# A two-layer decoder trunk on one core: one block-wise gate and up group, later sums, and a new order at the start of the first mixer

## The chip, the core and the metric

The kernel runs on one core of one Trainium2 chip. The core has a matrix engine, TensorE (PE in the profile; its weight loads are PEld), VectorE (DVE), ScalarE (ACT), GpSimd (POOL), and SyncE (SP), whose queue issues most of the transfers from and to HBM. The metric is the device time of one execution in microseconds (us); lower is better.

## What is computed

The input x has 256 tokens of 1024 columns, in float32. Two layers follow each other; each adds half a SwiGLU feed-forward network (FFN), a mixer, and half a second FFN, all on normed inputs. The first layer's mixer is dilated attention beside spatial gating, the second's is block-sparse attention. Cut to what matters here:

```python
def rms_norm(x, g):
    y = x * lax.rsqrt(jnp.mean(x * x, axis=-1, keepdims=True) + EPS)
    return y * g

def swiglu(x, w_gate, w_up, w_down):        # 1024 -> 2816 -> 1024
    return (jax.nn.silu(x @ w_gate) * (x @ w_up)) @ w_down

for layer in range(2):
    h = h + 0.5 * swiglu(rms_norm(h, ffn1_norm[layer]), ...)
    h = h + mixer[layer](rms_norm(h, mix_norm[layer]))
    h = h + 0.5 * swiglu(rms_norm(h, ffn2_norm[layer]), ...)
return rms_norm(h, final_norm)
```

## The kernel before

The code numbers six phases: 0 first FFN, 1 first mixer, 2 second FFN, 3 third FFN, 4 second mixer, 5 last FFN.

**Three products for one.** The matrix products must be as good as float32, so every operand is split in a high half (float32r, a rounded copy that ACT makes) and a low half (the rest, a subtraction on DVE). `mm3` (L388 to L391) then issues three products: high by high (L389), and the two mixed ones (L390, L391). Activations lie transposed, as `xTh` and `xTl`: 8 k tiles of 128 rows by 256 tokens. In a plain step the weights are stationary (128 x 128) and the 256 tokens move.

**The weight stream.** `weight_chunks` lists every piece of the weights in the order of use, and `Stream` brings them. A chunk has at most 2048 columns on 128 partitions (1 MB). SP loads it into one of three `raw` buffers (`load_one`, L202), ACT makes `whi` (L250) and DVE `wlo` (L257) in one of four pairs of buffers, and PE takes it (`take`) and gives it back (`free`). So a chunk can be split when PE has given back the one four places before it, and loaded when DVE has read the one three places before it. Where a chunk's `reset` is set, its first three k tiles are laid out with their column halves apart.

**An FFN.** The 2816 hidden columns are 11 groups of 256. Step n of 22 does the gate (n even) or up (n odd) columns of group n // 2: `colwise`, 2 column halves x 8 k tiles x 3 products. After every second step `gated` (L717 on) multiplies the gate by the row of inverse norms, applies SiLU, multiplies by up, and splits the result into `hTh` and `hTl`, 22 k tiles for the down projection that follows in 12 chunks.

**Blocks.** In phases 0, 3 and 5 part of the down projection runs by seven block products instead of eight, with sums of weight blocks (kind "S", formed by DVE at L264, L267 and L268 from the raw chunk) and sums of activation blocks (L739 to L741). There the weights move and 128 x 128 blocks of activations are stationary (`seven_products`). The last FFN's weight sums are formed ahead: `begin_sums` fetches a chunk into the tile `blocks` (L667), DVE forms three or four sums in place (L671 to L677), and `keep` stores them to HBM (L683). `AHEAD` names the steps of phases 2 and 3 at which the fetches are issued; the sums come one step after their fetch, and the store one step later. `blocks` has two buffers in phase 2.

**The start of a mixer.** `first_tiles` does four tiles of 256 columns: `LATE` (L537) is the order of the first two, `ps4[0]` and `ps4[1]`: six k tiles of the one, six of the other, then the last two of each. Four k tiles of `ps4[3]` follow, then (first mixer) `everywhere`: two products with ones (L482, L483) add the squares up, and a chain of DVE and ACT steps (mean L484, root L485, reciprocal L486, row L490) makes the row of inverse norms, by which `put_q` and `put_k` scale the queries and keys (L1068) for the first score (L1127). The next weight splits are tied behind the mean (`issue_after`).

The order of the instructions on each engine is drawn up by a scheduler at build time, by the order of the code and by what it takes to be ready; SP's queue works in order.

Of the kernel before, what the change touches and what calls it, by code (L numbers as in the profile page):

```python
# [10 lines left out]
F32 = mybir.dt.float32  # L11
# [4 lines left out]
S = 256  # L16
D = 1024
NT = S // 128
# [36 lines left out]
def weight_chunks():  # L55
# [11 lines left out]
    def ffn(name, layer, last=False, again=(2, 3), phase=None):  # L67
        first = len(chunks)
        wd = (f"{name}_w_down", layer)
        lag = LAGS.get(phase, FT)  # L70
        woven = phase in LAGS

        def seven(pair):
            add(wd, pair * 256, 2, 0, 512, MSHIFT, kind="S")

        for c in range(0, FF, 256):
            if len(chunks) == 0:
                for k in (0, 4):
                    add((f"{name}_w_gate", f"{name}_w_up", layer), k * 128, 4, c, c + 256, SHIFT,
                        (1, 2, 3) if k else (0.5, 1, 1.5, 2, 3))  # L80
                continue
            for m in ("gate", "up"):
                n = len(chunks)
                cuts = (6,) if first == 0 and n in again else ()
                cols((f"{name}_w_{m}", layer), c, 256, cuts,
                     RESET if n - first in again or woven and m == "gate" and c // 256 > lag else 0)
            if c // 256 >= lag:
                seven(c // 256 - lag)
        if last:
            for i in range(FT // 2):  # L90
                add(wd, i * 256, 2, 0, D, kind=LAST[i])
            return
        rest = list(range(FT // 2 - lag, FT // 2)) if woven else []
        behind = woven
        if lag > 2 and woven:
            seven(rest.pop(0))
        for c in range(512 if woven else 0, D, 256):
            for k, n in DOWN:
                add(wd, k * 128, n, c, c + 256, SHIFT, reset=RESET if behind or woven and lag == 2 and (c, k) == (768, 8) else 0)
                behind = bool(rest)  # L100
                if rest:
                    seven(rest.pop(0))
# [244 lines left out]
def trunk(ctx: ExitStack, tc: tile.TileContext, a, out):  # L347
# [311 lines left out]
    def begin_sums(fp, n):  # L659
# [29 lines left out]
    def ffn(phase):  # L689
        nonlocal nxt  # L690
        with tc.tile_pool(name="fp", bufs=1) as fp:
# [12 lines left out]
            else:  # L704
                parts = [fp.tile([128, S], F32R, name=n) for n in ("acch", "accl")]
                parts += [fp.tile([128, S], F32, name=n) for n in ("mean", "sqrt", "inverse")]

# [8 lines left out]

            ready, ahead = [], []  # L717

# [85 lines left out]
            for n in range(FT):  # L804
                k, m = n - n % 2, n % 2
                if phase == n == 0:
                    with tc.manual_schedule():
                        ready += begin(fp)
                elif phase or n > 1:
                    p = bank()  # L810
                    w = st.take()
                    colwise(p, w, *(() if n else (TURNS,)))
                    st.free()
                    ready.append(p)
                if phase == 2 and n == 1:

                    nc.tensor.matmul(bank()[:, :1], ones, ones[:, :1], start=True, stop=True)
                sums_at(n)
                if n == late - 1:
                    if phase not in (2, 5):  # L820
                        split(*parts[:2], nxt.acc[:, 0])
                    nxt.everywhere(*parts)
                    if last:
                        half = nxt.column(norm["half"], parts[3][:, :128], "halfcol")
# [7 lines left out]
                if n == late:  # L832
                    for i in range(0, n, 2):
                        gated(i, *ready[i : i + 2])
                elif n > late and m == 1:
                    gated(k, *ready[-2:])
# [386 lines left out]
    def first_tiles(put_q, put_k, step, places=None):  # L1223
# [11 lines left out]
        w = st.take()  # L1235
        tile_of(ps4[3], w, 1, range(4))
        if places:
# [7 lines left out]
        step()  # L1245
        tile_of(ps4[3], w, 1, range(4, KD))
        step()
# [164 lines left out]
def _layout(a):  # L1412
# [6 lines left out]
    for j, (ms, layer, r, n, c0, c1, *how) in enumerate(chunks):  # L1419
        w = np.concatenate([a[m][layer, r : r + n * 128, c0:c1] for m in ms], axis=1)  # L1420
        if j >= len(chunks) - FT // 2:
            w = w[:, ROWS]
        w = tiles(w)
        if how[-1] != "N":
# [38 lines left out]
```

## Time and profile before

| | |
|---|---|
| time, median of 3 runs | 919.52 us (919.25 to 919.65) |
| time of the profiled execution | 919.54 us |
| its span, first to last instruction | 917.8 us |
| mean granted TensorE clock | 0.999 |
| DMA, mean over the span | 220 GB/s, 202.17 MB |

The profile's page gives busy times by engine, a row of tenths over 40 equal slices of the span, the chain of work that ended last, and groups of instructions with count, busy time and mean duration. Products of PE are pipelined, so the duration of one (277 ns for 256 columns) is longer than the distance from one start to the next, and it is the distance that adds up.

### The profile page before, as it was taken

How to read it: one execution, taken by the hardware profiler on the slowest of the kernel's cores; microseconds unless marked ns; L12 is line 12 of the kernel's file. 1: busy time of each engine (PE TensorE's matmuls, PEld its weight loads, DVE VectorE, ACT ScalarE, POOL GpSimd, SP SyncE). 2: the span in 40 equal slices, each digit the busy share in tenths (PEclk: the TensorE clock that was granted, in tenths of full speed). 3: DMA queues.
4: the chain of work that ended last, by engine and by line, in shares of the span. 5: the costliest groups of instructions: out<-in, count | busy, mean ns of one | idle time of the engine just before them, and what ended most of it. 6: DMA issues, size and time to landing. Idle time of an engine off the chain costs nothing.

```text
span 917.8 us, 18462 instructions
## 1 busy us (share of the span) xinstructions
PE 910.5 (99%) x7531; PEld 891.8 (97%) x7531; DVE 774.5 (84%) x1267; ACT 561.9 (61%) x873; POOL 81.8 (9%) x117
## 2 busy tenths in 40 slices
PE   9999999999999999999999999999999999999997
PEld 9999999999999999999999999999999999999886
DVE  7999897997889777767799888878778799978897
ACT  7766555668667544444566555556777776555573
POOL 0000000034310000000000000001665100000001
PEclk9999999999999999999999999999999999999999
DMA  9656655665247779698746755575443566865691
GB/s 338 239 167 229 202 183 204 233 227 184 93 184 264 280 283 350 230 371 312 254 153 244 278 184 190 170 262 206 170 139 138 136 228 203 284 214 189 233 313 50
DMA packets 35428, 202.17 MB, mean 220 GB/s; under 512 B 4064, under 2 KB 6368, under 8 KB 14992
## 3 DMA queue, kind: packets, MB, share of 16 engines
q1 hardware_dynamic: 33840, 197.79, 60.4%
q0 software_dynamic: 496, 1.77, 0.9%
q10 hardware_dynamic: 1008, 1.44, 0.5%
q8 instruction: 59, 0.97, 0.4%
q14 instruction: 25, 0.20, 0.1%
HBM read 188.14 MB, written 12.85 MB: 219 GB/s over the span
## 4 chain that ended last, share of the span: by engine, by line
PE 99%; issue 0%; DVE 0%; POOLq 0%; POOL 0%; DVEq 0%
PE bank L391 31%; PE bank L389 31%; PE bank L390 31%; PE bank L1165 1%; PE bank L637 1%; PE bank L640 0%; PE bank L613 0%; PE bank L1127 0%; PE bank L1129 0%; PE bank L1128 0%; PE bank L923 0%; PE bank L919 0%; PE bank L920 0%; PE bank L1314 0%; PE bank L789 0%
## 5 line engine op out<-in xcount | busy, mean ns | idle before, releaser
L250 ACT ACTIVATE whi<-raw 128x1024 fp32r<-128x1024 f32 (+5 forms) x390 | 351.4, 946 | 227.1 <-PE bank L390 141.9
L257 DVE TENSOR_TENSOR wlo<-raw,whi 128x1024 fp32r<-128x1024 f32 (+5 forms) x390 | 414.5, 1091 | 36.1 <-ACT whi L250 34.9
L389 PE MATMUL bank<-xTh,whi 128*128 128x256 f32 x1600 | 442.8, 277 | 0.0
L390 PE MATMUL bank<-xTl,whi 128*128 128x256 f32 x1600 | 442.0, 276 | 0.0
L391 PE MATMUL bank<-xTh,wlo 128*128 128x256 f32 x1600 | 441.9, 276 | 0.0
L390 PEld LDWEIGHTS bank<-xTl,whi 128*128 128x128 f32 x1600 | 300.4, 188 | 0.2 <-DVE xTl L428 0.2
L389 PEld LDWEIGHTS bank<-xTh,whi 128*128 128x128 f32 x1600 | 300.4, 188 | 0.0
L391 PEld LDWEIGHTS bank<-xTh,wlo 128*128 128x128 f32 x1600 | 300.4, 188 | 0.0
L389 PE MATMUL bank<-hTh,whi 128*128 128x256 f32 x352 | 97.7, 278 | 0.0
L391 PE MATMUL bank<-hTh,wlo 128*128 128x256 f32 x352 | 97.3, 277 | 0.0
L390 PE MATMUL bank<-hTl,whi 128*128 128x256 f32 x352 | 97.3, 276 | 0.0
L390 PEld LDWEIGHTS bank<-hTl,whi 128*128 128x128 f32 x352 | 66.2, 188 | 0.0
L391 PEld LDWEIGHTS bank<-hTh,wlo 128*128 128x128 f32 x352 | 66.1, 188 | 0.0
L389 PEld LDWEIGHTS bank<-hTh,whi 128*128 128x128 f32 x352 | 66.1, 188 | 0.0
L724 DVE TENSOR_TENSOR hm<-gs,bank 128x512 f32<-128x512 f32 x44 | 29.9, 684 | 35.2 <-PE bank L391 35.0
L1060 POOL MEMSET k<- 64x256 f32 x12 | 3.3, 306 | 561.0 <-DVE x L439 560.8
L394 ACT ACTIVATE hSh<-gs 128x512 fp32r<-128x512 f32 (+1 forms) x31 | 18.6, 601 | 29.9 <-DVE gs L741 13.0
L389 PE MATMUL bank<-whi,hTh 128*128 128x256 f32 (+1 forms) x114 | 36.1, 316 | 0.0
L390 PE MATMUL bank<-wlo,hTh 128*128 128x256 f32 (+1 forms) x114 | 36.0, 316 | 0.0
L391 PE MATMUL bank<-whi,hTl 128*128 128x256 f32 (+1 forms) x114 | 36.0, 316 | 0.0
L389 PE MATMUL bank<-mixh,whi 128*128 128x256 f32 x128 | 35.7, 279 | 0.0
L721 DVE TENSOR_TENSOR gs<-bank,row 128x512 f32<-128x512 f32 x44 | 29.9, 686 | 6.9 <-PE bank L391 6.7
(247 smaller groups left out, 1308.7 us busy)
## 6 DMA issues: line engine op xcount, KB each, us to landing
raw<-in_weights SPq DMA_DIRECT2D x131, 1024.0 KB, 4.9
raw<-in_weights SPq DMA_DIRECT2D x28, 512.0 KB, 3.6
blocks<-in_weights SPq DMA_DIRECT2D x9, 1024.0 KB, 8.3
blocks<-blocks SPq DMA_DIRECT2D x9, 1024.0 KB, 7.2
raw<-blocks SPq DMA_DIRECT2D x7, 1024.0 KB, 4.8
raw<-in_weights SPq DMA_DIRECT2D x8, 768.0 KB, 5.0
raw<-in_weights SPq DMA_DIRECT2D x7, 256.0 KB, 4.8
blocks<-block SPq DMA_DIRECT2D x5, 256.0 KB, 8.9
```

The costliest lines, as they stand in the source:

```text
L250: done = nc.scalar.activation(hi, r, AF.Copy)
L257: self.made[u] = done, nc.vector.tensor_sub(lo, r, hi.bitcast(F32))
L389: nc.tensor.matmul(p, sh, mh, start=start, stop=False)
L390: nc.tensor.matmul(p, sh, ml, start=False, stop=False)
L391: return nc.tensor.matmul(p, sl, mh, start=False, stop=stop)
L394: return nc.scalar.activation(hi, src, AF.Copy), nc.vector.tensor_sub(lo, src, hi.bitcast(F32))
L637: nc.tensor.matmul(o, w[0][i][:, cs], xT[m][:, k], start=k == 0 and m == "h" and j % 2 == 0, stop=False)
L721: nc.vector.tensor_mul(g, both(pg), twice(norm["row"]))
L724: nc.vector.tensor_mul(hm, g, both(pu))
L1060: nc.gpsimd.memset(pair[j][o, 1].bitcast(F32), 0.0)
L1165: nc.tensor.transpose(tp[:, i * 128 : (i + 1) * 128], pr[:, i * 128 : (i + 1) * 128], ident)
```

## The change

The hidden group 7 of the second FFN goes by blocks. Its gate and up columns, once two chunks of 2048 columns, become four chunks of kind "S", each with two k tiles of gate and up side by side (1024 columns loaded). Its steps 14 and 15 become one call of `by_blocks`: for each of the four chunks seven `mm3` with the weights moving. The sums of activation blocks are made ahead by `forms` in steps 7 to 10, into parts of `hTh` and `hTl` that aren't used yet (`xS`). The result stands with tokens on the partitions; it is combined, gated by ACT with a column of norms (`token`), multiplied, transposed in 32 x 32 blocks by DVE, stored to HBM at step 16, loaded in the other layout at step 17, and split into `hT` at step 19. The next group's gate gets the layout of `reset`.

The sums for the last FFN come two steps behind their fetch, the store three steps behind. Their fetches move to other steps, `blocks` has one buffer, and four of the nine fetches use the tile `seven`, which also holds the block step's result and three scratch rows of `everywhere`.

In both mixers the last two k tiles of the first two tiles come in another order (`end_of`): first all products with the high half of the activations, then those with the low half. In the first mixer six k tiles of `ps4[3]`, not four, stand ahead of the products with ones.

```diff
-AHEAD = [(2, n) for n in (2, 5, 9, 12, 16, 19, 23, 26)] + [(3, 5)]
+AHEAD = [(2, n) for n in (1, 3, 6, 8, 16, 19, 22, 25)] + [(3, 5)]
+BORROWED = ((2, 3), (2, 8), (2, 19), (2, 25))
+BLOCKED = {2: (7,)}
...
+            if c // 256 in blocked:
+                for k in range(0, KD, 2):
+                    add((f"{name}_w_gate", f"{name}_w_up", layer), k * 128, 2, c, c + 256, MSHIFT, kind="S")
+                continue
...
-                     RESET if n - first in again or woven and m == "gate" and c // 256 > lag else 0)
+                     RESET if n - first in again or m == "gate" and (woven and c // 256 > lag or
+                                                                     c // 256 - 1 in blocked) else 0)
...
-    LATE = ((0, range(6)), (1, range(6)), (0, range(6, 8)), (1, range(6, 8)))
...
-        t = fp.tile([128, CH], F32, name="blocks", bufs=2 if AHEAD[n][0] == 2 else 1)
+        if AHEAD[n] in BORROWED:
+            t = fp.tile([128, 8, S], F32, name="seven").rearrange("p i s -> p (i s)")
+        else:
+            t = fp.tile([128, CH], F32, name="blocks")
...
+            def forms(i):
+
+                xg, t = (fp.tile([128, 2, S], F32, name="gs", bufs=2) for _ in range(2))
+                for j in range(2):
+                    nc.scalar.activation(xg[:, j], x1(2 * i + j), AF.Copy, scale=nxt.gain(2 * i + j))
+                f = t.rearrange("p i (t c) -> p (i t) c", t=2)
+                nc.vector.tensor_sub(f[:, :2], xg[:, 0].rearrange("p (t c) -> p t c", t=2), xg[:, :, 128:])
+                nc.vector.tensor_sub(f[:, 2], f[:, 1], xg[:, 0, :128])
+                nc.vector.tensor_add(f[:, 3], xg[:, 1, :128], f[:, 2])
+                split(*(h[:, i] for h in xS), f)
+
+            def by_blocks(m, n):
+
+                b = [bank() for _ in range(4)]
+                for c in range(KD // 2):
+                    w = st.take()
+                    a11, a12, a22 = [[xT[h][:, 2 * c + k, t * 128 : (t + 1) * 128] for h in "hl"]
+                                     for k, t in ((0, 0), (1, 0), (1, 1))]
+                    s3, s1, s2, s4 = ([h[:, c, i] for h in xS] for i in range(4))
+                    for (i, h), (sh, sl), q in (((2, 0), a11, 0), ((0, 0), a12, 2), ((1, 0), s4, 1), ((1, 1), a22, 6),
+                                                ((3, 0), s1, 3), ((0, 1), s2, 5), ((2, 1), s3, 4)):
+                        mm3(b[i][:, h * S : (h + 1) * S], sh, sl, w[0][q], w[1][q], c == h == 0,
+                            c == KD // 2 - 1 and (h == 1 or i == 3))
+                    if c < KD // 2 - 1:
+                        st.free()
+                t = fp.tile([128, 8, S], F32, name="seven")
+                nc.scalar.activation(t[:, 7], b[2][:, :S], AF.Copy)
+                nc.vector.tensor_add(t[:, 1:3], twice(t[:, 7]), both(b[0]))
+                nc.vector.tensor_add(t[:, 3], t[:, 2], b[2][:, S:])
+                nc.vector.tensor_sub(t[:, 0:6:5], twice(b[3][:, :S]), t[:, 2:4])
+                nc.vector.tensor_add(t[:, 4:7:2], t[:, 0:4:3], both(b[1]))
+                for i in range(NT):
+                    nc.scalar.activation(t[:, 1 + 5 * i], t[:, 1 + 5 * i], AF.Silu, scale=token[:, i : i + 1])
+                st.free()
+                nc.vector.tensor_mul(t[:, 2:4], t[:, 1:7:5], t[:, 4:6])
...
+                for i, f in ((2, store), (3, load), (5, take)):
+                    later[n + i] = f
...
             def sums_at(n):
 
+                if (phase, n - 2) in AHEAD:
+                    ahead[n - 2] = ahead[n - 2]()
+                if (phase, n - 3) in AHEAD:
+                    ahead.pop(n - 3)()
                 if (phase, n) in AHEAD:
-                    ahead.append(begin_sums(fp, AHEAD.index((phase, n))))
-                if (phase, n - 1) in AHEAD:
-                    ahead.append(ahead.pop()())
-                if (phase, n - 2) in AHEAD:
-                    ahead.pop()()
+                    ahead[n] = begin_sums(fp, AHEAD.index((phase, n)))
...
+                elif n // 2 in blocked:
+                    if m == 0:
+                        by_blocks(n // 2, n)
...
+                if n in later:
+                    later.pop(n)()
+                if blocked and 7 <= n < 11:
+                    forms(n - 7)
...
+    def end_of(ps, w, ks):
+
+        cs = [slice(j * 128, (j + 1) * 128) for j in range(2)]
+        for k in ks:
+            for j in range(2):
+                for m in range(2):
+                    nc.tensor.matmul(ps[j][:, :S], w[m][k][:, cs[j]], xT["h"][:, k], start=False, stop=False)
+        for k in ks:
+            for j in range(2):
+                nc.tensor.matmul(ps[j][:, :S], w[0][k][:, cs[j]], xT["l"][:, k], start=False, stop=k == KD - 1)
...
-        for j, ks in LATE:
-            tile_of(ps4[j], w, j, ks)
+        for j in range(2):
+            tile_of(ps4[j], w, j, range(6))
+        end_of(ps4, w, range(6, KD))
...
-        tile_of(ps4[3], w, 1, range(4))
+        ahead = 6 if places else 4
+        tile_of(ps4[3], w, 1, range(ahead))
...
-        tile_of(ps4[3], w, 1, range(4, KD))
+        tile_of(ps4[3], w, 1, range(ahead, KD))
```

More of the change, by code (lines that the diff above doesn't have):

```diff
@@ L705, in ffn @@
                 parts = [fp.tile([128, S], F32R, name=n) for n in ("acch", "accl")]
-                parts += [fp.tile([128, S], F32, name=n) for n in ("mean", "sqrt", "inverse")]
+                if phase in BLOCKED:
+                    seven = fp.tile([128, 8, S], F32, name="seven")
+                    parts += [seven[:, i] for i in range(3)]
+                else:
+                    parts += [fp.tile([128, S], F32, name=n) for n in ("mean", "sqrt", "inverse")]
             def turn_back(t):
@@ L715, in turn_back @@
                     nc.sync.dma_start(away[t], xn)
-            ready, ahead = [], []
+            ready, ahead, later = [], {}, {}
+            blocked = BLOCKED.get(phase, ())
+            xS = [h[:, FT - KD :].rearrange("p (i n) s -> p i n s", n=2).rearrange("p i n (t c) -> p i (n t) c", t=2)
+                  for h in hT]
+            def forms(i):
[7 more added lines that the diff above has]
+                split(*(h[:, i] for h in xS), f)
@@ new lines, in by_blocks, with store, load, take @@
+            def by_blocks(m, n):
[21 more added lines that the diff above has]
+                nc.vector.tensor_mul(t[:, 2:4], t[:, 1:7:5], t[:, 4:6])
+                flat = t.rearrange("p i s -> p (i s)")
+                turned, back = flat[:, 4 * S : 6 * S], flat[:, : 2 * S]
+                for i in range(NT):
+                    nc.vector.transpose(turned.rearrange("p (b t r) -> p b t r", t=NT, r=32)[:, :, i],
+                                        t[:, 2 + i].rearrange("p (b c) -> p b c", c=32))
+                kept = dram.tile([128, 512], F32, name=f"turned{phase}{m}")
+                def store():
+                    with tc.issue_after(st.last.ins):
+                        nc.sync.dma_start(kept, turned)
+                def load():
+                    for g in range(4):
+                        with tc.issue_after(st.last.ins):
+                            nc.sync.dma_start(back[32 * g : 32 * (g + 1)].rearrange("c (i f) -> c i f", i=4),
+                                              kept[:, 128 * g : 128 * (g + 1)].rearrange("(i c) f -> c i f", i=4))
+                def take():
+                    v = back.rearrange("p (i j t r) -> p j t i r", i=4, j=2, t=NT)
+                    for j in range(2):
+                        split(*(h[:, 2 * m + j].rearrange("p (t i r) -> p t i r", t=NT, i=4) for h in hT), v[:, j])
+                for i, f in ((2, store), (3, load), (5, take)):
+                    later[n + i] = f
@@ L822, in ffn @@
                     nxt.everywhere(*parts)
+                    if blocked:
+                        token = nxt.column(norm["row"], parts[3][:, :128], "halfcol")
                     if last:
@@ L834, in ffn @@
                         gated(i, *ready[i : i + 2])
-                elif n > late and m == 1:
+                elif n > late and m == 1 and n // 2 not in blocked:
                     gated(k, *ready[-2:])
@@ L1228, in first_tiles @@
         w = st.take()
-        for j, ks in LATE:
-            tile_of(ps4[j], w, j, ks)
+        for j in range(2):
+            tile_of(ps4[j], w, j, range(6))
+        end_of(ps4, w, range(6, KD))
         for _ in range(2):
@@ L1422, in _layout @@
             w = w[:, ROWS]
+        if how[-1] == "S" and len(ms) == 2:
+            w = w.reshape(-1, 2, 2, 4, 32).swapaxes(2, 3).reshape(w.shape)
         w = tiles(w)
```

1 line of the change is left out of this document (added).

## The prediction

> **What bounds the kernel now.** I read the page first: busy shares, then the granted clock, then the chain that ended last.
>
> ```profile
> PE 910.5 (99%) x7531; PEld 891.8 (97%) x7531; DVE 774.5 (84%) x1267; ACT 561.9 (61%) x873; POOL 81.8 (9%) x117
> ...
> PEclk9999999999999999999999999999999999999999
> ...
> PE 99%; issue 0%; DVE 0%; POOLq 0%; POOL 0%; DVEq 0%
> ...
> L389 PEld LDWEIGHTS bank<-xTh,whi 128*128 128x128 f32 x1600 | 300.4, 188 | 0.0
> ```
>
> TensorE (PE) is busy 99% of the span at full clock, and 99% of the chain is PE. Busy PE alone proves little, so the waits of its weight loads come next, then the one stretch that holds the second FFN, then the spacing of products there (pieces of the chain: start, length, both in us).
>
> ```profile
> PEld bank L1127 <- POOL k L1108: 0.3, 1, 0.3
> PEld bank L390 <- DVE xTl L428: 0.2, 1, 0.2
> ...
> 272.00:460.00 188.00, 188.00 (x1661) 188.00 (x1660) 142.32 (x176) 97.60 (x124) 0.00 (x0) 1.00 0.79 293
> ...
> 45 pieces in order of time: start us, us, what
> 349.95 0.11 PE bank L391
> ...
> 354.94 0.11 PE bank L390
> ```
>
> The reader is to see three things. PE waits twice after its start, 0.5 us in all, and both times in the first mixer. In the second FFN (272 to 460) PE never waits, while DVE is busy 142.32 of 188.00. And a product of 256 columns costs (354.94 - 349.95) / 44 = 0.1134 us there, its weight load hidden inside. So a product taken out of that stretch is worth 0.1134 us, and anything moved on DVE, ACT or SP is worth nothing until it makes PE wait.
>
> **The change, part by part.**
>
> **Block products.** Plainly, gate and up of group 7 are 2 matrices x 2 column halves x 8 k tiles x 3 terms = 96 products of 256 columns. In blocks, 4 pairs of k tiles x 7 x 3 = 84, also of 256 columns. Twelve go: 12 x 0.1134 = **-1.36 us**. This assumes that a block product (weights moving, activations stationary) costs the same. The third FFN has such products; these are starts of PE in the timeline:
>
> ```profile
> 591.51 0.28 PE L389 MATMUL bank<-whi,hTh 128*128 128x256 f32 x1
> ...
> 593.78 0.28 PE L391 MATMUL bank<-whi,hSl 128*128 128x256 f32 x1
> 593.90 0.28 PE L389 MATMUL bank<-hTh,whi 128*128 128x256 f32 x1
> ...
> 595.29 0.28 PE L389 MATMUL bank<-hTh,whi 128*128 128x256 f32 x1
> ```
>
> The 21 block products start (593.78 - 591.51) / 20 = 0.1135 apart. The next 12 plain ones are (595.29 - 593.90) / 12 = 0.116 apart, and then the old spacing is back. So going back to plain products costs about 12 x 0.0025 = 0.03; with rounding I take **+0.05**. [...] Ends: nothing, or, if all 84 ran at the 0.118 that the mixer's rows below show, +0.38. I stay by the third FFN's rows, which are the same operation.
>
> [...]
>
> **What the block form adds lies on DVE and ACT.** Durations of DVE by form (the last number before the bar's end is idle time):
>
> ```profile
> L257 DVE TENSOR_TENSOR wlo<-raw,whi 128x1024 fp32r<-128x1024 f32 x247 | 297.0, 1230 | 21.8 <-ACT whi L250 21.3
> L257 DVE TENSOR_TENSOR wlo<-raw,whi 128x768 fp32r<-128x768 f32 x37 | 34.9, 956 | 3.1 <-ACT whi L250 2.7
> L264 DVE TENSOR_TENSOR raw<-raw 128x512 f32<-128x512 f32 x22 | 15.1, 688 | 1.6 <-DMA raw<-in_weights 1.4
> L268 DVE TENSOR_TENSOR raw<-raw 128x256 f32<-128x256 f32 x22 | 9.3, 424 | 0.6
> L739 DVE TENSOR_TENSOR gs<-hm 128x256 f32<-128x256 f32 x22 | 9.2, 420 | 0.0
> L740 DVE TENSOR_TENSOR gs<-gs,hm 128x128 f32<-128x128 f32 x22 | 6.3, 286 | 0.0
> L394 DVE TENSOR_TENSOR hSl<-gs,hSh 128x512 fp32r<-128x512 f32 x22 | 15.1, 687 | 0.0
> L724 DVE TENSOR_TENSOR hm<-gs,bank 128x512 f32<-128x512 f32 x44 | 29.9, 684 | 35.2 <-PE bank L391 35.0
> ```
>
> A block chunk costs 0.956 + 1.230 + 0.688 + 2 x 0.424 = 3.72 us, four of them 14.9, where two plain chunks cost 4 x 1.23 = 4.9: +10.0. The sums of activations (forms) cost 0.42 + 2 x 0.286 + 0.687 = 1.68 each, four times: +6.7. Gathering the result takes four 512-wide steps and one of 256 (4 x 0.687 + 0.42), two transposes and two late splits of 256 columns (taken at 0.42 to 0.5 each, by the 256-wide rows): about 5.0, in place of 3 x 0.686 = 2.06: +2.9. The column of norms is two steps of 128 more, 0.6 by L740. That is +20 us on 142.3, against 186.6 of PE: the 45.7 us that DVE sits idle covers it on the whole, at a price of nothing. Where it is crowded is the first rival.
>
> SP gets a store and four reloads of the gathered group. They are needed only by the down projection, at least two steps of 5.44 us later. The store waits for DVE's transposes, and the raw loads queue behind it on SP:
>
> ```profile
> SPq L202 <- DVE wlo L257: 151.8, 36, 9.0
> ```
>
> In the window 270 to 470 SP's weight loads already wait for DVE 36 times, up to 9.0 us, and PE feels none of it; so I take this wait at nothing too, with the first rival's price if the cover is gone.
>
> **Sums two steps behind their fetch.** The same sums, stores and bytes, one step later, the second of each pair of buffers borrowed from the tile of the block step. The row they aim at:
>
> ```profile
> DVE blocks L671 <- DMA blocks<-in_weights: 11.9, 7, 2.8
> ```
>
> Up to 11.9 us of DVE idle go. DVE is not the bound and PE is never late here, so it is worth 0; it helps to pay for the 20 us above.
>
> **First mixer.** Pieces of the chain, then the timeline of DVE and POOL:
>
> ```profile
> 183.03 0.12 PE bank L391
> ...
> 187.39 0.12 PE bank L389
> 187.50 0.33 PE bank L390
> ...
> 188.07 0.16 PE bank L390
> ...
> 190.40 0.12 PE bank L482
> ...
> 190.86 0.12 PE bank L483
> ...
> 202.93 0.22 PE bank L1127
> ```
>
> ```profile
> 190.09 0.43 DVE L394 TENSOR_TENSOR mixl<-acc,mixh 128x256 fp32r<-128x256 f32 x1 [0.48 <-ACT mixh L394]
> ...
> 191.02 0.42 DVE L484 TENSOR_SCALAR qk<-bank 128x256 f32<-128x256 f32 x1 [0.51 <-PE bank L483]
> ...
> 201.97 0.74 POOL L1108 TENSOR_TENSOR k<-qk,k 64x256 fp32r<-64x256 f32 x1
> ```
>
> The spacing here is 0.118: 37 products from 183.03 to 187.39. At 187.50 and 188.07 PE waits for the low halves of the last two k tiles: 0.33 + 0.16 against 2 x 0.12, so 0.25. With the eight products that need only the high halves put first, the first low one comes six products (0.7 us) later: this wait goes, -0.25. But what is late next? The first score, L1127 at 202.93, starts 0.22 - 0.12 = 0.10 late already: it waits for POOL's k, done at 202.71, and that chain begins at the ones products L482 and L483. DVE sits idle 0.51 us for L483, because the next weight splits are tied behind the mean. So the score comes when L483 allows it, not when PE is free. L483 stands at 190.86 now: 12 products after the first chunk, then L482, then three more. With 18 ahead: the first chunk ends at 187.39 + 12 x 0.118 = 188.80, 18 products later it is 190.88 for L482, and L483 follows at 191.0 if the low half (done at 190.52) counts as ready, or at 191.35 behind three more products. The chain moves by +0.1 to +0.5, and the score with it. I take **+0.1**: the low half is done 0.36 us ahead of L482's new place, where it was late for the old one. The other end is -0.35 (both waits gone), if the score is issued behind further products. The second mixer gets the new order of the last k tiles too, but has no wait to remove (PE's two waits above are all): 0.
>
> **Sum.** -1.36 + 0.05 + 0.1 = -1.21. The profiled execution took 919.54 us (span 917.8 and 1.74 around it), the median of the runs is 919.52: 919.54 - 1.21 = **918.3 us**, 0.13% less. The bounds: -1.36 - 0.35 = -1.71, or 917.8; and -1.36 + 0.38 + 0.5 = -0.48, or 919.1.
>
> **The rivals.**
>
> *The block step starves PE (slower).* Place: the third and fourth block chunk and the gate of group 8. PE uses up a block chunk in 21 x 0.1134 = 2.38 us, DVE needs 3.72 for it. The weight buffers are four, so the fourth chunk can only be split when PE enters the first; by the end of the blocks, 9.52 us later, DVE must have done that chunk (3.72), the gate of group 8 (2.46) and the previous gating (2.06), 8.24 in all: it may start 1.28 us behind. How far behind it is:
>
> ```profile
> 314.42:347.06 32.64, 32.64 (x290) 32.64 (x289) 24.05 (x28) 15.29 (x18) 0.00 (x0) 1.00 0.80 302
> ```
>
> In the six steps before, DVE has 32.64 - 24.05 = 8.6 us idle, and forms (6.7) and three block chunks for plain ones (3 x 1.26 = 3.8) add 10.5: 1.9 behind, so PE would stall 0.6 if the gating comes first, and not at all if it waits, as its result isn't due for several steps. It ends above 919.5 once the stall passes 1.2 us, that is 2.5 us behind; at twice the computed lag (3.8) the stall is 2.5, and the time 918.3 + 2.5 = 920.8. For it: DVE is the busiest engine after PE. Against it: weights are split three steps ahead now, and the idle waits on blocks go.
>
> *The mixer's gain is kept.* If the score doesn't bind, -1.36 + 0.05 - 0.35: 917.9. For it: only 0.1 us of wait is seen there. Against it: that 0.1 shows that the chain already ends last.
>
> *Slower spacing.* Block products at 0.118, or the ones late by 0.5: 918.7. For it: plain products run at 0.118 for four us before 187.4. Against it: the third FFN's rows.
>
> *It doesn't do what it says.* Blocks issued, but an equal wait put in elsewhere: about 919.5. Nothing in the rows speaks for it.
>
> **How the numbers follow.** Forecast 918.3: 0.50. Gain kept, 917.9: 0.20. Slower spacing, 918.7: 0.15. Starved, 920.8: 0.10, of which 0.06 with a stall over 3.1 us. No gain, 919.5: 0.05. A measurement can tell about 0.2%, 1.84 us, from no change: faster means below 917.7, slower above 921.4. All terms at their best reach only 917.8, so faster gets 0.09 (from the gain-kept case and what I can't see); slower 0.06; within 0.2% 0.85. The range 917.6 to 919.3 holds the first three cases with their bounds and leaves out the starved one.
>
> **What would show it.** Right: in the second FFN PE still without waits, 12 products fewer, its stretch 1.3 us shorter; no wait on xTl (L428); the wait on POOL's k before the first score longer than 0.3; DVE's waits on blocks gone. Wrong: PE waiting for whi or wlo around the block step (first rival); the first score starting earlier than 202.9 (gain kept); block products over 0.115 apart.

## The result, and the profile after

The kernel after takes **929.78 us** (median of 4 runs, 927.90 to 934.21) against 919.59 us for the kernel before on the same chip (919.25 to 919.95): ratio of the means 1.0118, 95% interval 1.0079 to 1.0156. The forecast was 918.3 us. The kernel is slower by 1.2%, outside the range, and on the side to which the smallest chance was given. The profiled execution after took 930.96 us (span 929.2), 11.4 us of span more than before.

The page of the kernel after: busy time, the row of tenths of PE, its granted clock, and the chain that ended last. In the code after, the three products of `mm3` are L397 to L399, the splits L258 (ACT) and L265 (DVE), the sums L681 to L687, a pair of the down projection leaves PE's bank at L446 and L447, and `xTh` and `xTl` are L433 and L436.

```profile
PE 914.2 (98%) x7519; PEld 894.5 (96%) x7519; DVE 788.9 (85%) x1310; ACT 571.7 (62%) x893; POOL 81.5 (9%) x117
...
PE   9999999999999999999699999999999999999997
...
PEclk9999999999999999999899999999999999999999
...
PE 76%; DVE 11%; DMA 8%; issue 2%; ACT 1%; SPq 1%; POOL 0%; POOLq 0%; DVEq 0%; ACTq 0%
```

The twelve products are gone (7531 to 7519). But one slice of PE, the twentieth of 40 (441 to 465 us), has fallen to 6, with the clock at 8, and DVE and DMA together now hold 19% of the chain that held 99% PE before. PE's waits over the whole span have one large entry:

```profile
PE bank L397 <- ACT xTh L433: 7.0, 1, 7.0
PE bank L620 <- PEq L1551: 0.8, 1, 0.8
PE bank L398 <- DVE xTl L436: 0.4, 1, 0.4
```

The place, in the timelines of PE, ACT and DVE (start, length, line; in brackets the idle time before and who ended it):

```profile
455.31 0.28 PE L399 MATMUL bank<-xTh,wlo 128*128 128x256 f32 x1
462.62 0.58 PE L397 MATMUL bank<-xTh,whi 128*128 128x256 f32 x1 [7.03 <-ACT xTh L433]
```

```profile
457.25 2.00 ACT L258 ACTIVATE whi<-raw 128x1024 fp32r<-128x1024 f32 x2 [3.59 <-DMA raw<-in_weights]
...
462.06 0.91 ACT L433 ACTIVATE xTh<-x,gT 128x256 fp32r<-128x256 f32 x2 [0.31 <-DVE x L447]
```

```profile
458.33 2.36 DVE L265 TENSOR_TENSOR wlo<-raw,whi 128x1024 fp32r<-128x1024 f32 x2 [3.24 <-ACT whi L258]
460.61 0.68 DVE L446 TENSOR_TENSOR part<-bank,half 128x512 f32<-128x512 f32 x1
461.33 0.69 DVE L447 TENSOR_TENSOR x<-part,x 128x512 f32<-128x512 f32 x1
```

This is the seam between the second and the third FFN. The last column pair of the down projection has left PE by 451.3, and the third FFN's first products use the k tiles that are ready. At 455.31 PE needs the last ones. They wait for an addition on DVE (L446, L447) that takes 1.4 us and whose data have long been there. It stands in DVE's order behind the split of a weight chunk, and that split waits until 458.33 for a chunk that came late from memory. So a late weight, which PE itself didn't yet need, holds up an addition that PE did need.

What follows the stall is in these windows (busy time and instructions of PE, PEld, DVE, ACT, POOL, then granted clock, DMA share, GB/s):

```profile
455.00:460.00 5.00, 0.59 (x6) 0.39 (x4) 1.76 (x3) 2.27 (x3) 0.00 (x0) 0.84 0.99 405
460.00:465.00 5.00, 1.97 (x7) 1.68 (x8) 4.96 (x8) 3.17 (x5) 0.00 (x0) 0.50 0.66 252
465.00:470.00 5.00, 5.00 (x31) 5.00 (x30) 3.94 (x6) 2.32 (x3) 0.00 (x0) 0.63 0.31 105
470.00:475.00 5.00, 5.00 (x45) 5.00 (x44) 2.33 (x5) 1.94 (x2) 0.00 (x0) 1.00 0.59 215
```

PE returns at half clock (0.50), is at 0.63 in the next window, and back at 1.00 by 470. Three rows more, by groups of products: the third FFN's first 96 products and the next 192, after; and those 192 before.

```profile
451.35:472.93 21.58, 14.14 (x99) 13.65 (x97) 13.99 (x18) 9.77 (x12) 0.00 (x0) 0.76 0.73 284
473.16:495.78 22.62, 22.62 (x195) 22.62 (x193) 20.85 (x32) 15.38 (x20) 0.00 (x0) 1.00 0.37 126
```

```profile
452.25:463.13 10.88, 10.88 (x99) 10.88 (x98) 9.40 (x14) 5.65 (x8) 0.00 (x0) 1.00 0.50 155
463.35:485.11 21.76, 21.76 (x194) 21.76 (x193) 20.65 (x32) 15.29 (x20) 0.00 (x0) 1.00 0.45 163
```

This is the account of the loss. The third FFN begins at 451.35 instead of 452.25, 0.90 us early: 1.29 saved (the product that starts at 440.08 started at 441.37 before), and 0.39 lost around a short wait for `wlo` at 441.6 (the 0.3 in the row below). Its first 96 products take 21.58 us instead of 10.88: 10.70 lost, 7.20 of them idle and 3.50 by the low clock and the wait on `xTl`. The next 192 take 22.62 instead of 21.76, at full clock and with no wait: 0.86 lost, and 96 more from 498.25 on take 11.31 where 96 x 0.1134 = 10.9 would be expected, 0.40 lost. The sum, -0.90 + 10.70 + 1.26 = 11.06, leaves 0.3 of the 11.4 us. The two rows for the small terms, a group of the page and a window, both of after:

```profile
L399 PEld LDWEIGHTS bank<-hTh,wlo 128*128 128x128 f32 x352 | 66.1, 188 | 0.3 <-DVE wlo L265 0.3
```

```profile
498.25:509.56 11.31, 11.31 (x98) 11.31 (x97) 10.58 (x17) 5.34 (x7) 0.00 (x0) 1.00 0.75 275
```

Why the chunk came late is in DVE's waits in the second FFN (270 to 460), which the forecast had expected to vanish, and in the row of ACT:

```profile
DVE seven L681 <- DMA seven<-in_weights: 12.1, 2, 6.8
DVE blocks L681 <- DMA blocks<-in_weights: 12.0, 3, 6.8
...
ACT whi L258 <- DMA raw<-in_weights: 40.4, 15, 6.8
```

The sums now wait 24.1 us for their fetches, where the sums of before waited 11.9; and ACT waits 40.4 us for weight chunks, where before none of its waits in this stretch is put down to one. One of the waits of the sums, in DVE's timeline, with what stands around it, and behind it the lines of ACT and SP in that time:

```profile
412.71 1.22 DVE L265 TENSOR_TENSOR wlo<-raw,whi 128x1024 fp32r<-128x1024 f32 x1
420.74 0.69 DVE L681 TENSOR_TENSOR blocks<-blocks 128x512 f32<-128x512 f32 x1 [6.81 <-DMA blocks<-in_weights]
...
423.40 4.09 DVE L265 TENSOR_TENSOR wlo<-raw,whi 128x1024 fp32r<-128x1024 f32 x4
```

```profile
414.49 2.01 ACT L258 ACTIVATE whi<-raw 128x1024 fp32r<-128x1024 f32 x2 [2.15 <-DMA raw<-in_weights]
...
425.79 0.33 SPq L210 DMA_DIRECT2D raw<-in_weights  x1
```

And DMA over the same stretch, 404 to 428, in 40 slices of 0.6 us: busy tenths of the 16 engines, and GB/s.

```profile
DMA  9999400094799986999999999999996300000737
GB/s 427 393 416 382 205 27 27 0 150 68 246 396 341 246 232 273 423 437 423 423 437 423 420 423 416 362 437 430 430 440 259 150 27 27 0 0 0 82 68 177
```

DVE does nothing for 6.81 us, while DMA is busy nine tenths or more (slices 16 to 29, from 413.6 to 422, at 362 to 440 GB/s). One raw chunk has landed by 414.49, when ACT begins its high half. Its low half isn't formed before 423.40, since DVE's next instruction is the sum; the other two raw buffers are waiting for loads that land behind the fetch. So no raw buffer comes free, SP issues no load until 425.79, and when the transfers under way have landed DMA falls to nothing (the zeros from 423.2 on) while DVE catches up. SP's queue works in order too: the sums are formed by 422.88, but their store is issued at 426.16, directly behind the load of 425.79. Then the same begins again for the last sum, at 439.31 (6.83 us). Two shorter waits of the same kind stand ahead of these, 4.64 us up to 383.28 and 5.26 us up to 403.38. Each turn of this loop costs the stream of weights some 4 us of DMA (an estimate from the rows of 404 to 444 at `e11_nowait` below, for two turns: 40 x (0.96 - 0.77) = 7.6), and the last one ends at the seam.

### The profile page after: what moved, and what is told of

The parts are those of the page before. It is cut to its first block, busy times and chain, and to the rows that moved or that the text cites. A ratio compares the mean times of both kernels' runs of the same rounds, so it can differ in the third digit from the quotient of the medians.

```text
span 929.2 us, 18516 instructions
## 1 busy us (share of the span) xinstructions
PE 914.2 (98%) x7519; PEld 894.5 (96%) x7519; DVE 788.9 (85%) x1310; ACT 571.7 (62%) x893; POOL 81.5 (9%) x117
## 4 chain that ended last, share of the span: by engine, by line
PE 76%; DVE 11%; DMA 8%; issue 2%; ACT 1%; SPq 1%; POOL 0%; POOLq 0%; DVEq 0%; ACTq 0%
PE bank L398 24%; PE bank L399 24%; PE bank L397 24%; DVE wlo L265 6%; DMA raw<-in_weights 4%; DMA seven<-in_weights 2%; ACT whi L258 1%; DMA turned<-seven 1%; PE bank L1251 1%; DMA blocks<-in_weights 1%; PE bank L644 1%; DVE hTl L402 0%; DVE gs L798 0%; DVE xTl L436 0%; PE bank L647 0%
## 5 line engine op out<-in xcount | busy, mean ns | idle before, releaser
L258 ACT ACTIVATE whi<-raw 128x1024 fp32r<-128x1024 f32 (+5 forms) x395 | 354.8, 942 | 193.9 <-PE bank L398 103.3
L265 DVE TENSOR_TENSOR wlo<-raw,whi 128x1024 fp32r<-128x1024 f32 (+5 forms) x395 | 418.2, 1086 | 34.8 <-ACT whi L258 33.5
L397 PE MATMUL bank<-xTh,whi 128*128 128x256 f32 x1560 | 434.2, 278 | 7.0 <-ACT xTh L433 7.0
L398 PE MATMUL bank<-xTl,whi 128*128 128x256 f32 x1560 | 433.3, 278 | 0.4 <-DVE xTl L436 0.4
L399 PE MATMUL bank<-xTh,wlo 128*128 128x256 f32 x1560 | 433.2, 278 | 0.0
L397 PEld LDWEIGHTS bank<-xTh,whi 128*128 128x128 f32 x1560 | 294.6, 189 | 7.3 <-ACT xTh L433 7.2
L398 PEld LDWEIGHTS bank<-xTl,whi 128*128 128x128 f32 x1560 | 294.2, 189 | 0.7 <-DVE xTl L436 0.7
L399 PEld LDWEIGHTS bank<-xTh,wlo 128*128 128x128 f32 x1560 | 294.4, 189 | 0.0
L397 PE MATMUL bank<-hTh,whi 128*128 128x256 f32 x352 | 97.8, 278 | 0.0
L399 PE MATMUL bank<-hTh,wlo 128*128 128x256 f32 x352 | 97.5, 277 | 0.1
L399 PEld LDWEIGHTS bank<-hTh,wlo 128*128 128x128 f32 x352 | 66.1, 188 | 0.3 <-DVE wlo L265 0.3
L397 PEld LDWEIGHTS bank<-hTh,whi 128*128 128x128 f32 x352 | 66.2, 188 | 0.0
L801 DVE TENSOR_TENSOR hm<-gs,bank 128x512 f32<-128x512 f32 x43 | 29.1, 681 | 21.9 <-PE bank L399 21.7
L397 PE MATMUL bank<-whi,hTh 128*128 128x256 f32 (+1 forms) x130 | 40.6, 312 | 0.0
L398 PE MATMUL bank<-wlo,hTh 128*128 128x256 f32 (+1 forms) x130 | 40.5, 312 | 0.0
L399 PE MATMUL bank<-whi,hTl 128*128 128x256 f32 (+1 forms) x130 | 40.5, 312 | 0.0
L799 ACT ACTIVATE gs<-gs 128x512 f32<-128x512 f32 x43 | 26.7, 623 | 16.5 <-DVE gs L798 16.5
L397 PE MATMUL bank<-mixh,whi 128*128 128x256 f32 x128 | 35.8, 280 | 0.0
```

Of the source, the lines that this page charges most:

```text
L258: done = nc.scalar.activation(hi, r, AF.Copy)
L265: self.made[u] = done, nc.vector.tensor_sub(lo, r, hi.bitcast(F32))
L397: nc.tensor.matmul(p, sh, mh, start=start, stop=False)
L398: nc.tensor.matmul(p, sh, ml, start=False, stop=False)
L399: return nc.tensor.matmul(p, sl, mh, start=False, stop=stop)
L799: nc.scalar.activation(g, g, AF.Silu)
```

## The experiments

Times are compared with runs of the kernel before on the same chip (919.95 to 920.00 us). The edits are on the kernel after, where nothing else is said.

**Which part is it?** First the two parts alone and the block step with the old sums.

`e1_noblocks`, the sums' new steps and the mixer without the block step:

```
-BLOCKED = {2: (7,)}
+BLOCKED = {}
```

> The whole change without the block products (group 7 as plain gate and up). Theory A (the crowd that the block step makes on DVE from 331 to 358 us makes the weight loads late, and they stay late to the end of the second FFN): the 7 us wait of PE for xTh goes, about 919.6. Theory B (the new steps and places of the sums alone make the loads late): the wait stays, 924 to 929.

920.44 us, ratio 1.0005 (0.9996 to 1.0015): no change.

`e2_oldsums`, the block step and the mixer, with the fetches at the old steps, sums and stores one and two behind, and two buffers of their own:

```
-AHEAD = [(2, n) for n in (1, 3, 6, 8, 16, 19, 22, 25)] + [(3, 5)]
-BORROWED = ((2, 3), (2, 8), (2, 19), (2, 25))
+AHEAD = [(2, n) for n in (2, 5, 9, 12, 16, 19, 23, 26)] + [(3, 5)]
+BORROWED = ()
...
-            t = fp.tile([128, CH], F32, name="blocks")
+            t = fp.tile([128, CH], F32, name="blocks", bufs=2 if AHEAD[n][0] == 2 else 1)
...
+                if (phase, n - 1) in AHEAD:
+                    ahead[n - 1] = ahead[n - 1]()
                 if (phase, n - 2) in AHEAD:
-                    ahead[n - 2] = ahead[n - 2]()
-                if (phase, n - 3) in AHEAD:
-                    ahead.pop(n - 3)()
+                    ahead.pop(n - 2)()
```

> The whole change with the sums for the last FFN as before: old fetch steps, one step behind, two buffers of their own. Theory A: the block step's crowd is there all the same, so the loads stay late, 924 to 929. Theory B: the wait goes, about 918.3.

918.59 us, ratio 0.9985 (0.9975 to 0.9994), 1.4 us faster than before, with no PE wait in the second FFN or at the seam. So block step and mixer without the moved sums give what was forecast for them, and the moved sums without the block step do no harm. The loss needs both.

`e3_mixer`, the new order of products in the mixers, put into the kernel before:

```
-        for j, ks in LATE:
-            tile_of(ps4[j], w, j, ks)
+        for j in range(2):
+            tile_of(ps4[j], w, j, range(6))
+        end_of(ps4, w, range(6, KD))
...
-        tile_of(ps4[3], w, 1, range(4))
+        ahead = 6 if places else 4
+        tile_of(ps4[3], w, 1, range(ahead))
```

> The kernel before with the new start of the mixers alone. My prediction's step: +0.1, at most +0.5 (the first score waits for the chain from the ones products); the rival that the gain is kept: -0.35. Theories A and B say nothing on it: 919.2 to 920.0 either way, with no wait on xTl and a longer wait on POOL's k.

919.85 us, ratio 0.9995 (0.9986 to 1.0005): it can't be told from nothing.

**Is the seam the whole loss?** `e4_hold` keeps the splits of the next weights behind the last addition of the down projection:

```
+                    hold = phase == 2 and c == 3
+                    if hold and k0 == 8:
+                        st.hold()
                     if k0 + n == FT:
-                        nxt.pair(c, b, row, fp)
+                        made = nxt.pair(c, b, row, fp)
+                        if hold:
+                            st.release(tc, made)
```

> The whole change, but the weight splits that stand before the last x addition of the second FFN on DVE are held back until it is done. Theory C (PE waits because that addition is queued on DVE behind a split whose load is late; the weights that PE needs next are there): the 7 us wait and the slow clock after it go, 918 to 919.5, with the loads as late as before. If instead the weights themselves are late, PE waits for whi or wlo in the third FFN: 922 or more.

922.09 us (919.27 to 926.62), ratio 1.0024 (1.0009 to 1.0039), so more is left than the 918 to 919.5 expected. The 7-us wait is gone, and with it 8.1 of the 10.2 us between the medians. The weights are as late as in the kernel after (the last four sums wait 4.2 to 7.0 us for their fetches), and it is now the two products with ones that stand behind the splits. PE's waits, and DVE at that place:

```profile
PE bank L490 <- ACT acch L402: 1.1, 1, 1.1
PE bank L491 <- DVE accl L402: 1.1, 1, 1.1
```

```profile
457.83 7.33 DVE L265 TENSOR_TENSOR wlo<-raw,whi 128x1024 fp32r<-128x1024 f32 x6 [0.87 <-ACT whi L258]
465.08 0.42 DVE L402 TENSOR_TENSOR accl<-acc,acch 128x256 fp32r<-128x256 f32 x1
```

So the place of the stall can be moved. Its cause, the lateness, lies earlier.

**What makes the stream late?** Six edits of the new sums and of the block step's work. First the lag, and the steps of the last two fetches.

`e5_lag1`, sums one and stores two steps behind, at the new steps and with the borrowed tile (the last hunk of `e2_oldsums` alone):

> The whole change, but the sums one step behind their fetch and the store two, with the new steps and the borrowed tile. Theory D (with fetches three steps apart and the store three steps behind, each fetch stands on SP directly behind the store of the one before, which waits for DVE's sums, which wait for that fetch: a loop of fetch, sums, store of 17 to 18 us against 15 us that PE takes for three down chunks, so what the block step lost is not won back but grows): the wait goes, 918.3 to 919.3. Theory E (the borrowed tile or the steps themselves do it): it stays, 923 or more.

926.41 us, ratio 1.0071 (1.0051 to 1.0091). The stall at the seam is gone here too, but a part of the loss has another form. The waits of PE, and the stretch 370 to 460, first of this kernel, then of before:

```profile
PE bank L398 <- DVE wlo L265: 0.9, 1, 0.9
PE bank L620 <- PEq L1551: 0.8, 1, 0.8
PE bank L398 <- DVE xTl L436: 0.6, 1, 0.6
```

```profile
370.00:460.00 90.00, 90.00 (x766) 90.00 (x765) 65.86 (x84) 44.02 (x56) 0.00 (x0) 1.00 0.83 307
```

```profile
370.00:460.00 90.00, 90.00 (x797) 90.00 (x796) 64.46 (x80) 42.79 (x54) 0.00 (x0) 1.00 0.79 295
```

The first wait is in the block step, at 356: the place of the first rival. From 370 to 460 PE has no gap and full clock, but issues 766 products in 90 us instead of 797: 31 x 0.113 = 3.5 us. With about 2.6 us of gaps and the 1.3 saved, 4.8 of the 6.0 us of span over before are explained; 0.7 more lie ahead of the second FFN. The expectation (918.3 to 919.3, by a loop of fetch, sums and store on SP) failed: the lag of two steps isn't the sole cause, and the shorter lag is no remedy.

`e6_steps`, the last two fetches one step later, at 23 and 26:

> The whole change, but the last two fetches one step later (23 and 26, as before), sums and stores still two and three steps behind. Theory D: one more step between a store and the fetch behind it at 19 to 23 gives the loop five more us, so part or all of the lag is won back: 918.3 to 922. Theory E with the borrowed tile as the cause: 927 or more, as the change.

926.21 us, ratio 1.0068 (1.0051 to 1.0085); the wait at the seam is 5.3 us. This is a smaller loss of the same kind, and above the 918.3 to 922 that the loop on SP called for.

`e7_own`, two buffers of their own in place of the borrowed tile (`BORROWED = ()`, and `bufs=2` as above):

> The whole change, but the fetches have two buffers of their own and borrow no tile. Theory D: the order on SP stays, so the time stays, 925 to 930. Theory E with the borrowed tile as the cause: 918.3 to 919.3.

928.86 us, ratio 1.0102 (1.0087 to 1.0117), wait at the seam 7.1 us. The borrowed tile isn't the cause.

`e8_early`, own buffers and lag of two, with the first four fetches at the old steps 2, 5, 9, 12:

> The change with its first four fetches at the old steps (2, 5, 9, 12) and two buffers of its own; the last four at the new steps, sums two steps behind. Theory F (forms, two sets of sums and the block chunks' sums come together on DVE between 320 and 356 us, so the weights fall two to three chunks behind before the block step, and with a fetch every three steps from then on nothing is won back): one set of sums leaves that stretch, the wait is gone or short, 918.3 to 922. Theory G (the last four fetches, or the two steps between fetch and sums, do it): 925 to 929, as with own buffers and the new steps (928.9).

919.69 us (one execution of ten at 925.03, the others 918.65 to 920.66), ratio 1.0003 (0.9990 to 1.0016). In the profiled execution, 920.66 us, the seam is free; one wait is left, earlier, behind the block step:

```profile
PE bank L399 <- DVE wlo L265: 1.3, 1, 1.3
```

`e9_noforms`, without the sums of activations (the block products use plain blocks of x, so the second FFN's output isn't the reference's):

```
-                    s3, s1, s2, s4 = ([h[:, c, i] for h in xS] for i in range(4))
+                    s3, s1, s2, s4 = a11, a12, a22, a11
...
-                if blocked and 7 <= n < 11:
-                    forms(n - 7)
```

> The change without forms: the sums of activation blocks are left out, and the products that use them take plain blocks of xT instead, so group 7 is wrong and the products are as many. It takes 4 x 1.68 = 6.7 us of DVE out of the stretch before the block step. Theory F: the wait goes, 918 to 920. Theory G: 925 to 930.

926.28 us, ratio 1.0071 (1.0056 to 1.0086), wait at the seam 5.9 us. Taking 6.7 us of DVE's work out of the crowd ahead of the block step gives back 3.9 of the 10.2 us, where the expectation that this crowd makes the loss called for all of it (918 to 920).

`e10_eight`, own buffers, and only the fourth fetch moved, from step 8 to 12:

> The change with two buffers of its own and one fetch moved from step 8 to step 12, so its sums (2.7 us of DVE) come with the block step and not with the forms; all else as in the change. Theory F: shorter by about the 2.7 us and what follows from it, 918.5 to 925. Theory G: 927 to 930.

921.07 us (918.52 to 925.19), ratio 1.0020 (1.0006 to 1.0035). The same program runs 6.7 us apart from one execution to the next. The only one with a profile is a long one, 925.04 us, with 3.3 us of wait at the seam; that the short ones have no stall is likely, but not shown. Fetch, sums and splits seem to be close to a balance here that a few us tip.

So nothing that the change added in work is the cause by itself. What goes along with the loss is the wait of the last four groups' sums for their fetches. Added up, it is 23.5 us in the kernel after (6.8 twice), 19.0 to 23.2 in the other runs with a stall at the seam (`e6_steps`, `e7_own`, `e9_noforms`, `e10_eight`), 21.9 in `e4_hold` and 16.8 in `e5_lag1`; and 7.4 in the kernel before and 10.8, 6.9 and 3.5 in `e1_noblocks`, `e2_oldsums` and `e8_early`, of which none is measurably slower than before. But `e3_mixer` has 15.8 us of it, four waits of 3.7 to 4.3 us, and loses nothing. So such a wait is not a loss in itself; waits up to 4.3 us pass unseen where the block step hasn't crowded DVE first. The last two runs take the wait away and leave the rest.

`e11_nowait`: the last four groups' sums (fetches at 16, 19, 22 and 25) do the same instructions, at nearly the same places of DVE's order, on a tile of zeros, so that they wait for nothing. The fetched chunk is stored unsummed, so the last FFN's weights aren't the reference's.

```
+        if n in (4, 5, 6, 7):
+            if n == 4:
+                stale.append(fp.tile([128, CH], F32, name="stale"))
+                nc.gpsimd.memset(stale[0], 0.0)
+            u = stale[0]
+        else:
+            u = t
-        b22, b12, b11, b21 = (t[:, i * 512 : (i + 1) * 512] for i in range(4))
+        b22, b12, b11, b21 = (u[:, i * 512 : (i + 1) * 512] for i in range(4))
...
+                if u is not t:
+                    behind.enter_context(tc.issue_after(st.made[max(st.made)][1].ins))
```

> The kernel after, but the sums of the last four groups of this FFN (fetches at steps 16, 19, 22, 25) work in place on a tile of zeros of their own, with the same instructions at the same places of VectorE's order; the fetched group is stored as it came (so the last FFN's weights are wrong). VectorE's work, the fetches, stores and reloads stay; only VectorE's wait for the fetch (4.6, 5.3, 6.8 and 6.8 us in the kernel after) goes. Theory of the wait (VectorE stands in front of a late fetch while weights that have landed are not split, their raw buffers stay taken and SyncE cannot load on): the 7 us of PE before the third FFN go, 918.5 to 921 us. Rival, the deficit from before the block step (2 to 3 chunks behind at 350 us, whatever comes later): PE still stands 4 us or more, 924 to 929.

918.49 us, ratio 0.9987 (0.9977 to 0.9996). No wait of PE is left but the one at the start. DVE at the place of the wait shown above, and DMA over the same 404 to 428:

```profile
409.51 1.22 DVE L265 TENSOR_TENSOR wlo<-raw,whi 128x1024 fp32r<-128x1024 f32 x1
410.64 0.68 DVE L696 TENSOR_TENSOR stale<-stale 128x512 f32<-128x512 f32 x1
...
412.70 0.68 DVE L700 TENSOR_TENSOR block<-stale 128x512 f32<-128x512 f32 x1
413.30 2.35 DVE L265 TENSOR_TENSOR wlo<-raw,whi 128x1024 fp32r<-128x1024 f32 x2
```

```profile
DMA  9999999999999999999859369997899989999989
```

Here it is the same work in the same order: DVE goes on to the next split at 413.30, and DMA never falls to zero. Over 404 to 444 it moves more than in the kernel after, first after, then this one:

```profile
404.00:444.00 40.00, 39.91 (x352) 39.71 (x352) 26.12 (x34) 15.78 (x21) 0.00 (x0) 1.00 0.77 285
```

```profile
404.00:444.00 40.00, 40.00 (x355) 40.00 (x354) 31.56 (x41) 20.32 (x27) 0.00 (x0) 1.00 0.96 356
```

`e12_pool`: the same four groups' sums done by GpSimd (POOL), which then waits for the fetch in DVE's place.

```
+            eng = nc.gpsimd if n in (4, 5, 6, 7) else nc.vector
-            nc.vector.tensor_sub(b12, b22, b12)
+            eng.tensor_sub(b12, b22, b12)
...
```

> The kernel after, with the sums of the last four groups on GpSimd instead of VectorE; the output is the reference's. VectorE loses 14 subtractions and additions (9.6 us) and the wait for the fetch; the wait moves to GpSimd, which has nothing else to do there. Theory of the wait: as in the run without the wait, 918.5 to 921 us, no PE wait over 1 us. Rival of the deficit from before the block step: 924 to 929. If GpSimd's sums are so slow that the store and the reload come late, a PE wait shows in the last FFN instead.

918.83 us, ratio 0.9986 (0.9977 to 0.9996), no PE wait but the one at the start. POOL in its timeline:

```profile
413.86 1.34 POOL L682 TENSOR_TENSOR blocks<-blocks 128x512 f32<-128x512 f32 x1 [9.74 <-DMA blocks<-in_weights]
415.28 2.15 POOL L683 TENSOR_TENSOR blocks<-blocks 128x512 f32<-128x512 f32 x1
```

The wait is still there, 9.74 us of it, and the sums take up to three times as long (2.15 us against 0.69). But nothing is queued behind it. It isn't free for DVE either: its splits of 1024 columns over 370 to 440, first in `e11_nowait`, then in this run, have a mean of 1216 and 1413 ns.

```profile
L265 DVE TENSOR_TENSOR wlo<-raw,whi 128x1024 fp32r<-128x1024 f32 x22 | 26.2, 1216 | 0.0
```

```profile
L265 DVE TENSOR_TENSOR wlo<-raw,whi 128x1024 fp32r<-128x1024 f32 x21 | 29.1, 1413 | 5.8 <-ACT whi L258 5.8
```

With the wait off DVE, all three parts of the change together beat the kernel before by 0.14%. `e2_oldsums` does so as well, at 0.15%, and the two can't be told apart.

`e11_nowait` keeps DVE's work and frees the stores from the sums. `e12_pool` keeps the stores behind the sums and takes fifteen operations off DVE (not fourteen, as expected), but with the longer splits DVE's busy time over the program is no shorter: 790.4 us against 788.9 in the kernel after. What both take away is the wait at the head of DVE's queue.

The rival in these two runs was that the stream is behind from before the block step, whatever comes later. It falls: both runs leave everything before step 16 as it is, and have no stall. What `e9_noforms` and `e10_eight` give back shows that being behind there helps the loss on; it doesn't make it.

## Why the prediction was wrong, point by point

**The block step's saving: right.** In the kernel after, its products and the first one after them start at

```profile
348.92 0.28 PE L397 MATMUL bank<-whi,xTh 128*128 128x256 f32 x1
...
358.44 0.28 PE L397 MATMUL bank<-xTh,whi 128*128 128x256 f32 x1
```

84 products in 9.52 us, 0.1133 each, as taken from the third FFN's rows. The first 12 plain ones behind them start (359.84 - 358.44) / 12 = 0.117 apart, where the third FFN had 0.116. `e2_oldsums` gives the sum, -1.4 us for block step and mixer together, where -1.21 was forecast.

**The mixer: right in its mechanism.** The wait on `xTl` in the mixer is gone from PE's waits (the first product with a low half comes seven products later, not six as reckoned, which changes nothing), and the one on POOL's k grew from 0.3 to 0.5:

```profile
PEld bank L1213 <- POOL k L1194: 0.5, 1, 0.5
```

The second score product starts at 203.04 after and at 202.99 before, 0.05 later; +0.1 was taken. `e3_mixer` agrees that nothing is won.

**The block step's work on DVE and SP at nothing: right only with the old sums.** In `e2_oldsums` it is at nothing. In the kernel after it is not. The 20 us taken for DVE were on the high side: its busy time over the program grew by 14.4 us (774.5 to 788.9).

**The sums: wrong, and this is the step that failed.** The prediction said "Up to 11.9 us of DVE idle go. DVE is not the bound and PE is never late here, so it is worth 0; it helps to pay for the 20 us above." The idle time did not go but doubled, to 24.1 us, and its long pieces became the cause of the 10.2 us lost. Two things were left out. First, a sum two steps behind its fetch in the code isn't two steps behind on DVE. The scheduler still put it in front of splits whose chunks land before the fetch does, and the fetch had not landed when DVE came to it: 6.8 us of idle ahead of it, twice. (The one shown above was issued by SP at 408.67, DVE was ready for its sum at 413.93, and it had landed at 420.74.) Second, DVE's idle time wasn't slack that other work could use. While DVE waits for a fetch, splits that could run stand behind it, raw buffers stay taken, and SP's loads stop (the zeros in the DMA row). The pair of `e11_nowait` and the kernel after shows it: the split that starts at 413.30 in the one starts only at 423.40 in the other, behind the sums that began at 420.74 after 6.81 us without work. With the wait taken off DVE in `e11_nowait` and `e12_pool`, the loss is gone. The prediction added DVE's busy time up against 188 us, and asked of its one waiting instruction only how long it waits, not who is queued behind it.

**The first rival: the right kind, at the wrong place and price.** It looked for the stall at the third and fourth block chunk and the gate of group 8, at 0.6 to 2.5 us, with 0.10. In the kernel after, PE goes through those without a wait. The stall came 100 us later, at the seam, because a few us of delay pass unseen while the buffers hold (DVE's waits of 4.64 and 5.26 us up to 403.38 show in no wait of PE), and come due where PE needs something of DVE at once. There it cost 7.2 us, and 3.5 and 1.3 more for the low clock and the slower products behind it, which no rival had priced. In `e5_lag1` and `e8_early` waits of 0.9 and 1.3 us did come at or close behind the block step.

**The chances.** 0.85 for no change leaned on "PE is never late here". This was true of the kernel before, and said nothing of how near it was to waiting: `e10_eight`, where executions of one and the same program spread from 918.5 to 925.2 us, suggests how small the reserve is once the change is in.

**What stays open.** The scheduler's order follows from the steps of the fetches in a way that wasn't worked out. Why the first four fetches' steps decide the wait of the last ones (`e8_early`) is seen, not explained. How late the stream must be for a wait of some 4 us to cost anything wasn't measured. It wasn't tried whether the last sums, kept on DVE and put one split later, would do as well as on POOL.

## What to carry to other kernels

Before work that waits for a transfer is put on an engine, list what is queued behind it and which buffers and loads hang on that. Here it stood on the engine that frees the buffers of the weight stream, and 6.81 us of wait put a split off by 10.1 us (413.30 to 423.40). Try such work on an engine with nothing else to do: here that paid (ratio 0.9986 to the kernel before, against 1.0118), though a sum took up to three times as long (2.15 us against 0.69) and DVE's splits beside it slowed by a sixth (1413 ns against 1216). That PE was busy 99% of the time in the kernel before, with no wait in the second FFN, didn't show how small its reserve was: look for that in how far ahead the stream is at the next place where the engine needs a result at once.

## What the runs showed of the hardware

**The stall of 7.2 us cost half as much again.** In the kernel after, PE idle for 7.2 us came back with a granted clock of 0.50 and had full clock again about 6 us after its first product (0.63 over 465 to 470 is half clock for 3.7 of the 5 us), with 3.5 us lost, some 0.4 of them to the wait on `xTl`. From 464.20 to 468.68 its products start 21 in 4.48 us, 0.213 apart instead of 0.113. In the other runs with a stall at the seam (3.3 to 7.1 us) the products behind it come mostly 0.213 us apart too, until 4.1 us (`e6_steps`, `e10_eight`), 4.8 (`e7_own`) and 5.9 (`e9_noforms`) after the first one; their granted clock over 460 to 470 is 0.75, 0.83, 0.66 and 0.66 in that order. So the way back to full clock took 4.1 to 6.1 us in these five runs. PE wasn't busy throughout: 1.97 of the first 2.38 us in the kernel after.

**After some of the stalls the products stayed slower at full clock.** In the rows of 473.16 to 495.78 the 192 products are 22.62 / 192 = 0.1178 apart instead of 0.1133, with no wait shown. This ended by itself at about 513 in the kernel after, and lasted from 370 to 460 at least in `e5_lag1`, behind gaps of 1.2 and 0.4 us, until a gap of 0.8 us at 461. In the other runs with a stall at the seam the spacing was 0.113 again once the clock was back. The prediction met the same 0.118 in the first mixer and took it for a property of the place. What sets it off and ends it stays open.
